# The first four feature pairs of each feed-forward layer as two 512-wide projections in two halves, in a four-layer decoder trunk

## The chip, the cores and the metric

The kernel is one program on one core of a Trainium2 chip. It takes one sequence of 256 tokens with 1024 channels through four residual layers. The metric is the device time of one execution in microseconds (us), lower is better. The kernel before takes 1203.94 us (median of 3 runs, 1202.83 to 1204.53).

The engines named here: TensorE (PE in the rows; PEld is its weight load), VectorE (DVE), ScalarE (ACT), GpSimd (POOL) and SyncE (SP, which issues the loads). Each works its own instructions off in order and waits on semaphores for the others.

## The reference, cut to what matters

Four layers, each a token mixer (attention, spatial gating, state-space, attention) and a feed-forward part. The change is in the feed-forward part:

```python
def conv_gated_ffn(xn, w_up, conv_w, conv_b, w_down):      # xn 256 x 1024, w_up 1024 x 5632
    h = causal_depthwise_conv(xn @ w_up, conv_w, conv_b)   # 3 taps over the tokens, per feature
    a, g = jnp.split(h, 2, axis=-1)                        # 2816 + 2816 features
    return (jax.nn.silu(g) * a) @ w_down                   # w_down 2816 x 1024

for i in range(DEPTH):
    xn = rmsnorm(x, norm_g[i, 0])
    m = ...                                                # mixer of this layer
    x = x + m
    x = x + conv_gated_ffn(rmsnorm(x, norm_g[i, 1]), ...)
return rmsnorm(x, final_norm_g)
```

## The kernel before

**Products in three.** Every weight chunk is a 128x2048 fp32 tile. ScalarE copies each half of it to a rounded high part `wh` (L85), VectorE subtracts to get the low part `wl` (L86), and a product is three matmuls: high by high, and the two mixed ones. The activations have such parts too, `xth` and `xtl` (1024 channels in 8 k-tiles by 256 tokens). `Weights` loads chunks ahead of use, and `step`, `prep_to` and `half_to` set how many are split ahead; the halves stand in the queues of ScalarE and VectorE between the other work.

**A feed-forward layer (class `FFN`).** Its 2816 feature pairs are 22 groups of 128 (`NM`), called u0 to u21 here; the chunk of a group holds the 128 `a` and 128 `g` columns for all 8 k-tiles. A group is projected *feature-major* (`proj_feat`): the weights are the stationary operand and the 256 tokens stream, 48 matmuls of 256 columns (L138 to L140), and the result, features by tokens, lies in one PSUM bank. Then `evac` takes it: two ScalarE activations with the middle tap and the bias (L432), four VectorE multiply-adds for the other two taps, reading the bank again (L436), then SiLU (L442), the product (L443) and the split for the next product (L212, L213). Each pair of groups is one chunk of the down product (d0 to d10, `down`, 24 matmuls of 512 columns, L146 to L148). The order of the body is u3, u4, u5, d0, u6, u7, d1, u8, u9, d2 and so on; `pend` delays the `evac` of a group to the round after its projection.

**The head.** The first three groups are projected *token-major* (`proj_tok`): the tokens of one block of 128 (block 0 or 1) are stationary and the 256 weight columns stream, so that block 0 can start while the norm of block 1 is still on its way. Two groups go to one bank (7 for block 0, 2 for block 1), the third to half of another (4 and 3). ScalarE copies these results to SBUF (`tk`, L388 and L389), and in the middle of u3 twelve transposes (L394) turn them into features by tokens in banks 4, 5 and 6, where `evac` finds them as it would u-groups.

**PSUM.** There are eight banks. Banks 0 to 3 are the accumulators of the down product from d0 on; banks 4 to 7 take the groups: group u*a* from u3 on goes to bank 4 + *a* mod 4, so u3 7, u4 4, u5 5, u6 6, u7 7. A matmul or transpose into a bank waits until the last reader of its former contents is done, and for a group that is the last of its four multiply-adds.

**Around the head.** `K.run` runs `tail(1)` of the phase before, the norm of block 1 (Square on ScalarE L165, power on GpSimd L177, scale on VectorE L169), then `head(0)`, which after its second chunk calls the transposes of block 1 (`xt_tr`, L193) and their evacuation (L199, L200), two more chunks are split, `head(1)`, one more chunk, and `body`. The attention phase already has a head of the other kind (`proj_half`, L236): 512 columns of half of the k-tiles per chunk.

The state-space layer (`S5`) uses `FFN.head` and `FFN.transposes` for its own input product.

Of the kernel before, what the change touches and what calls it, by code (L numbers as in the profile page):

```python
# [8 lines left out]
F32 = mybir.dt.float32  # L9
F32R = mybir.dt.float32r  # L10
BF16 = mybir.dt.bfloat16
AF = mybir.ActivationFunctionType
# [3 lines left out]
D = 1024  # L16
EPS = 1e-6
NM = 22
# [334 lines left out]
class FFN(Phase):  # L353
# [10 lines left out]
    def open(self):  # L364
        self.tmp = self.pool("ffn", 3)
        self.nc.scalar.preload_act_table_set("silu_and_others")
        self.cw = self.tmp.tile([128, 2, NM, 4], F32, tag="cw", bufs=1, name="cw")
        self.nc.sync.dma_start(self.cw[:, :, :, :], self.k.ins["conv"][self.i])
        self.bg = self.k.s5.stage(self.tmp) if self.k.s5 and self.k.s5.done else iter(())
        self.gt = {}  # L370
        self.acc = [[self.k.bank(2 * b + h) for h in range(2)] for b in range(2)]
        self.resid = self.k.add_acc(self.acc)
        self.hb = [(7, 4), (2, 3)]

    def head(self, b, mid):
        k = self.k
        if b == 0:
            self.hn = [k.w.take() for _ in range(3)]
        for c in range(3):
            p = k.bank(self.hb[b][c // 2])  # L380
            k.proj_tok(self.hn[c], b, p[:, 256 * (c % 2):256 * (c % 2) + 256])
            if c == 1:
                mid()
        if b == 0:
            self.tk = []
        tk = k.xn_p.tile([128, D], F32, tag="xn", name="tk")
        self.tk.append(tk)
        self.nc.scalar.activation(tk[:, 0:512], k.bank(self.hb[b][0]), AF.Copy)  # L388
        self.nc.scalar.activation(tk[:, 512:768], k.bank(self.hb[b][1])[:, 0:256], AF.Copy)  # L389

    def transposes(self, m, p):
        for b in range(2):
            for s in range(2):
                self.nc.tensor.transpose(p[:, 256 * s + 128 * b:256 * s + 128 * b + 128],  # L394
                                         self.tk[b][:, 256 * m + 128 * s:256 * m + 128 * s + 128],
                                         self.k.ident[:, :])

    def body(self):
        k, w = self.k, self.k.w
        pend = []  # L400
        for kind, a in self.order()[3:-3]:
            n = w.take()
            if kind == "u":
                p = k.bank(4 + a % 4)
                k.proj_feat(n, p, 0)
                if a == 3:
                    for m in range(3):
                        self.transposes(m, k.bank(4 + m))
                        pend.append((m, k.bank(4 + m)))
                k.proj_feat(n, p, 1)  # L410
                e = [(a, p)]
            else:
                k.down(self.gt[a], n, self.acc, (0, 1), a == 0, False)
                e = []
            self.evac(pend)
            pend = e
            w.step()
            for _ in range(1 + (kind == "d" and a % 2)):
                next(self.bg, None)
        self.evac(pend)  # L420
        for _ in self.bg:
            pass
# [339 lines left out]
class S5(Phase):  # L762
# [340 lines left out]
    def open(self):  # L1103
# [12 lines left out]
        nc.gpsimd.memset(self.kk[0][:, :, :, :], 0.0)  # L1116
        self.gt = {}

    def head(self, b, mid):
        FFN.head(self, b, mid)  # L1120
        if b == 0:
            k, w = self.k, self.k.w
            w.prep_to(w.use + 3)
            w.dma_to(w.use + 9)
            self.t0 = k.big.tile([128, D], F32, tag="gb", name="t0")
            for r in range(2):
                self.nc.sync.dma_start(self.t0[:, 512 * r:512 * r + 512], self.d_t[r][:, 0:512])
        else:
            self.k.w.prep_to(self.k.w.use + 6)

    def body(self):
        k, nc, w = self.k, self.nc, self.k.w
        ut = k.pst[:, 4:8, :].rearrange("p b (a t) -> p (b a) t", a=2)
        n = w.take()
        k.proj_feat(n, k.bank(7), 0)
        for m in range(3):
            FFN.transposes(self, m, k.bank(4 + m))
        k.proj_feat(n, k.bank(7), 1)
        tabs = [w.take() for _ in range(5)]
        TT = []  # L1140
        for i, tag in enumerate(("xth", "xtl")):
            t = k.big.tile([128, 2048], F32, tag=tag, name=f"T{i}")
# [149 lines left out]
        n = w.take()  # L1292
# [41 lines left out]
def pack(x, norm_g, final_norm_g, sb_w_qkv, sb_w_o, sg_w_in, sg_norm_g, sg_w_s, sg_b, sg_w_o,  # L1334
         ssm_w_in, ssm_lam_re, ssm_lam_im, ssm_log_dt, ssm_b_re, ssm_b_im, ssm_c_re, ssm_c_im,
         ssm_d, ssm_w_glu, ffn_w_up, ffn_conv_w, ffn_conv_b, ffn_w_down):

    c = np.ascontiguousarray
    a = {}
    a["x"] = x.reshape(2, 128, D)  # L1340
    a["g"] = np.concatenate([norm_g.reshape(8, D), final_norm_g.reshape(1, D), sg_norm_g.reshape(1, D)])
    a["up"] = c(ffn_w_up.reshape(4, 8, 128, 2, NM, 128).transpose(0, 4, 2, 1, 3, 5)).reshape(4, NM, 128, 2048)
    a["down"] = c(ffn_w_down.reshape(4, ND, 2, 128, D).transpose(0, 1, 3, 2, 4)).reshape(4, ND, 128, 2048)
    cv = np.concatenate([ffn_conv_w, ffn_conv_b[:, None]], axis=1)
    a["conv"] = c(cv.reshape(4, 4, 2, NM, 128).transpose(0, 4, 2, 3, 1))
    w = sb_w_qkv.reshape(2, 8, 128, 3, 8, 128)
    a["wqk"] = c(w[:, :, :, 0:2].transpose(0, 4, 2, 1, 3, 5)).reshape(2, 8, 128, 2048)
    w = sb_w_qkv[:, :, 2048:].reshape(2, 2, 4, 128, 2, 512)
    a["wv"] = c(w.transpose(0, 4, 1, 3, 2, 5)).reshape(2, 4, 128, 2048)
    a["wo"] = c(sb_w_o.reshape(2, 4, 2, 128, D).transpose(0, 1, 3, 2, 4)).reshape(2, 4, 128, 2048)  # L1350
    w = sg_w_in.reshape(8, 128, 2, 1024)
    a["sgu"] = c(w[:, :, 0].reshape(8, 128, 4, 2, 128).transpose(2, 1, 0, 3, 4)).reshape(4, 128, 2048)
    a["sgv"] = c(w[:, :, 1].reshape(2, 4, 128, 2, 512).transpose(3, 0, 2, 1, 4)).reshape(4, 128, 2048)
    a["sgo"] = c(sg_w_o.reshape(4, 2, 128, D).transpose(0, 2, 1, 3)).reshape(4, 128, 2048)
    a["sgws"] = c(sg_w_s[0].transpose(2, 0, 1))
    a["sgb"] = sg_b.reshape(1, D)
    w = ssm_w_in.reshape(8, 128, 4, 2, 128)
    a["ssin"] = c(w.transpose(2, 1, 0, 3, 4)).reshape(4, 128, 2048)
    w = ssm_w_glu.reshape(4, 2, 128, 2, 2, 512)
    a["glu"] = c(w.transpose(4, 0, 2, 1, 3, 5)).reshape(8, 128, 2048)  # L1360
    p = [ssm_lam_re[0], ssm_lam_im[0], np.broadcast_to(ssm_log_dt[0][:, None], (64, 64))]
    a["spar"] = c(np.stack([v.reshape(32, 128).T for v in p], axis=1))
    p = (ssm_b_re[0], ssm_b_im[0], ssm_c_re[0].transpose(0, 2, 1), ssm_c_im[0].transpose(0, 2, 1))
    a["sbc"] = c(np.stack([v.reshape(32, 2, 64, 16).transpose(1, 2, 0, 3) for v in p], axis=2)).reshape(128, 4, 512)
    v = np.stack([v.reshape(32, 2, 64, 16).transpose(1, 3, 0, 2) for v in p[:2]], axis=2).reshape(32, 2, 2048)
    a["sbt"] = c(np.tile(v, (4, 1, 1)))
    a["sd"] = c(ssm_d.reshape(8, 4, 32).transpose(1, 0, 2))
    a["e32"] = np.tile(np.eye(32, dtype=np.float32), (4, 1))
    i = np.arange(128)
    v = np.stack([i // 16 % 2, i // 64], axis=1)  # L1370
    a["own"] = c(np.stack([v[:, n] == g for n in range(2) for g in range(2)], axis=1).astype(np.float32))
    a["le"] = (i[:, None] <= i[None, :]).astype(np.float32)
    ge = (i[:, None] >= i[None, :]).astype(np.float32)
    one = np.ones((128, 128), np.float32)
    a["tri"] = np.concatenate([-ge, -one, np.float32(-1e30) * np.eye(128, dtype=np.float32), ge, ge], axis=1)
    a["ident"] = np.eye(128, dtype=np.float32)
    return a
# [28 lines left out]
```

## Time and profile before

| | |
|---|---|
| time, median of 3 runs | 1203.94 us |
| profiled execution: its own time | 1204.05 us |
| its span, first to last instruction | 1202.3 us |
| TensorE busy (matmul) | 1180.3 us, 98% |
| VectorE busy | 892.8 us, 74% |
| ScalarE busy | 709.4 us, 59% |
| feature-major matmuls of 256 columns (L138 to L140) | 4656, 283 to 284 ns each from start to modelled end |
| matmuls of 512 columns of the down products and their like (L146 to L148 on `gh`, `gl`) | 1536, 389 to 393 ns each |
| weights read | 222.27 MB from HBM, 196 GB/s over the span |

A matmul's duration in the profile runs to its modelled end and overlaps the next; what a stream of them costs is read from the distance between starts in the timeline. The number in brackets at the end of a timeline row is how long the engine had been idle before it, and which instruction ended that. Rows of equal instructions that follow each other are merged, with their count behind x.

### The profile page before, as it was taken

Reading aid. Unit: us, or ns where it says so; the run is one execution under the profiler, and the core shown is the slowest. Engines: PE = TensorE matmul, PEld = TensorE weight load, DVE = VectorE, ACT = ScalarE, POOL = GpSimd, SP = SyncE. Lnnn points to the kernel's source line nnn. Section 1 sums busy time; section 2 is a strip of 40 time slices with the busy share of each in tenths; the row PEclk is TensorE's granted clock in tenths of the full one; section 3 lists DMA queues with packets and bytes.
Section 4 is the critical chain, followed back from the end, with each engine's and each line's share of the span. In section 5 each row is a group of like instructions: output and inputs, shape, how many; then the busy total and the mean of one; then the engine's idle time right before and its main releaser. Section 6 shows DMA issues by size and latency. Waiting matters only on the chain. (4 is left out here: it accounts for less than half of the span.)

```text
span 1202.3 us, 22001 instructions
## 1 busy us (share of the span) xinstructions
PE 1180.3 (98%) x9076; PEld 1078.8 (90%) x9076; DVE 892.8 (74%) x1273; ACT 709.4 (59%) x1080; POOL 150.8 (13%) x293
## 2 busy tenths in 40 slices
PE   9999999999999999999987999999999999999997
PEld 5898999999898999999976899999988989999996
DVE  6665689799767699899569759777765656886673
ACT  6565576557564564667466657555545655665551
POOL 3894000000186001000100000000000000000000
PEclk9999999999999999999999999999999999999999
DMA  7633368787655456677762746644535333564530
GB/s 276 229 107 123 138 217 284 231 308 250 247 210 188 154 220 220 226 265 263 315 246 72 267 150 218 227 176 175 200 139 205 106 124 122 202 240 178 208 123 35
DMA packets 49416, 236.94 MB, mean 197 GB/s; under 512 B 14882, under 2 KB 15778, under 8 KB 24099
## 3 DMA queue, kind: packets, MB, share of 16 engines
q1 hardware_dynamic: 46066, 223.21, 51.6%
q0 software_dynamic: 3104, 12.06, 2.5%
q8 instruction: 71, 1.16, 0.4%
q14 instruction: 31, 0.25, 0.1%
q10 hardware_dynamic: 144, 0.26, 0.1%
HBM read 222.27 MB, written 13.24 MB: 196 GB/s over the span
## 5 line engine op out<-in xcount | busy, mean ns | idle before, releaser
L86 DVE TENSOR_TENSOR wl<-raw,wh 128x1024 fp32r<-128x1024 f32 x343 | 412.3, 1227 | 56.6 <-ACT wh L85 56.6
L138 PE MATMUL pst<-xth,wh 128*128 128x256 f32 x1552 | 441.0, 284 | 0.0
L139 PE MATMUL pst<-xtl,wh 128*128 128x256 f32 x1552 | 439.1, 283 | 0.0
L140 PE MATMUL pst<-xth,wl 128*128 128x256 f32 x1552 | 439.1, 283 | 0.0
L85 ACT ACTIVATE wh<-raw 128x1024 fp32r<-128x1024 f32 x343 | 349.4, 1048 | 8.4 <-DMA raw<-in_up_dram 4.2
L138 PEld LDWEIGHTS pst<-xth,wh 128*128 128x128 f32 x1552 | 297.7, 192 | 2.3
L139 PEld LDWEIGHTS pst<-xtl,wh 128*128 128x128 f32 x1552 | 297.8, 192 | 1.2
L140 PEld LDWEIGHTS pst<-xth,wl 128*128 128x128 f32 x1552 | 297.7, 192 | 0.0
L436 DVE SCALAR_TENSOR_TENSOR y<-pst,cw,y 128x255 f32<-128x255 f32 x352 | 160.7, 479 | 72.8 <-ACT y L432 66.6
L146 PE MATMUL pst<-wh,gh 128*128 128x512 f32 x512 | 201.3, 393 | 0.0
L147 PE MATMUL pst<-wl,gh 128*128 128x512 f32 x512 | 199.8, 390 | 0.0
L148 PE MATMUL pst<-wh,gl 128*128 128x512 f32 x512 | 199.4, 389 | 0.0
L432 ACT ACTIVATE y<-pst,cw 128x256 f32<-128x256 f32 x176 | 88.2, 557 | 69.4 <-PE pst L140 64.8
L148 PEld LDWEIGHTS pst<-wh,gl 128*128 128x128 f32 x512 | 96.1, 188 | 20.4
L146 PEld LDWEIGHTS pst<-wh,gh 128*128 128x128 f32 x512 | 96.2, 188 | 19.4 <-issue 0.3
L147 PEld LDWEIGHTS pst<-wl,gh 128*128 128x128 f32 x512 | 96.3, 188 | 18.4 <-DVE wl L86 0.2
L147 PE MATMUL pst<-wl,xth 128*128 128x256 f32 (+1 forms) x336 | 105.5, 314 | 1.3 <-DVE wl L55 1.0
L146 PE MATMUL pst<-wh,xth 128*128 128x256 f32 (+1 forms) x336 | 106.1, 316 | 0.0
L148 PE MATMUL pst<-wh,xtl 128*128 128x256 f32 (+1 forms) x336 | 105.4, 314 | 0.0
L177 POOL TENSOR_TENSOR r<-m,mhalf 128x1 f32<-128x1 f32 x20 | 11.1, 554 | 741.0 <-DVE m L175 732.5
L212 ACT ACTIVATE gh<-y 128x256 fp32r<-128x256 f32 x88 | 36.1, 418 | 75.2 <-DVE y L443 75.2
L442 ACT ACTIVATE y<-y 128x256 f32<-128x256 f32 x88 | 36.3, 419 | 73.7 <-DVE y L436 73.7
(173 smaller groups left out, 1203.0 us busy)
## 6 DMA issues: line engine op xcount, KB each, us to landing
raw<-in_up_dram SPq DMA_DIRECT2D x88, 1024.0 KB, 4.9
raw<-in_down_dram SPq DMA_DIRECT2D x44, 1024.0 KB, 4.9
raw<-in_wqk_dram SPq DMA_DIRECT2D x16, 1024.0 KB, 5.1
raw<-in_wo_dram SPq DMA_DIRECT2D x8, 1024.0 KB, 4.8
raw<-in_glu_dram SPq DMA_DIRECT2D x8, 1024.0 KB, 6.7
raw<-in_wv_dram SPq DMA_DIRECT2D x7, 1024.0 KB, 6.0
gb<-in_g_dram SPq DMA_DIRECT2D x8, 512.0 KB, 5.7
d_gt<-gf POOLq DMA_DIRECT2D x4, 1024.0 KB, 7.4
```

The lines of the kernel that those rows point to most:

```text
L85: nc.scalar.activation(h[:, s], r[:, s], AF.Copy)
L86: nc.vector.tensor_tensor(out=l[:, s], in0=r[:, s], in1=h[:, s], op=ALU.subtract)
L138: nc.tensor.matmul(out, h[:, cols], xh, start=first, stop=False, skip_group_check=True)
L139: nc.tensor.matmul(out, h[:, cols], xl, start=False, stop=False, skip_group_check=True)
L140: nc.tensor.matmul(out, l[:, cols], xh, start=False, stop=last, skip_group_check=True)
L146: nc.tensor.matmul(out, ah, h[:, cols], start=first, stop=False, skip_group_check=True)
L147: nc.tensor.matmul(out, ah, l[:, cols], start=False, stop=False, skip_group_check=True)
L148: nc.tensor.matmul(out, al, h[:, cols], start=False, stop=last, skip_group_check=True)
L212: self.nc.scalar.activation(g[0][:, j], src, AF.Copy)
L432: nc.scalar.activation(y[:, cs], p[:, cs], AF.Identity, scale=cw[:, s, m, 2:3], bias=cw[:, s, m, 3:4])
L436: nc.vector.scalar_tensor_tensor(y[:, o + tap:o + 256], p[:, o:o + 256 - tap], cw[:, s, m, 2 - tap:3 - tap], y[:, o + tap:o + 256], ALU.mu ...
L442: nc.scalar.activation(y[:, 256:512], y[:, 256:512], AF.Silu)
```

## The change

The head of a feed-forward layer takes the first *four* groups token-major, as two blocks of 512 columns (groups 0 and 1, groups 2 and 3), each in two chunks: chunk 0 and 1 hold the k-tiles 0 to 3 and 4 to 7 of the first block, chunk 2 and 3 of the second (`pack` lays the weights out so). `head` runs chunks 0 to 2 with `proj_half`, 12 matmuls of 512 columns each per token block, and copies the finished bank (7 or 2) to `tk` after the second. The fourth chunk, in the place where u3's chunk was, is run in `body` by `rest`, for block 0 (bank 4) and block 1 (bank 3). Between the two stand the transposes of groups 0 and 1 into banks 5 and 6; those of groups 2 and 3 into banks 4 and 5 stand in the middle of u4. The bank of a later group changes: u4 takes bank 7, and from u5 on group u*a* takes 4 + (*a* - 3) mod 4, so u5 6, u6 7, u7 4. `evac` takes groups 0 and 1 after the fourth chunk, 2 and 3 after u4, 4 after u5. The state-space layer keeps the old head under the name `narrow`.

```diff
+        self.vb = [(7, 4), (2, 3)]
     def head(self, b, mid):
         k = self.k
         if b == 0:
             self.hn = [k.w.take() for _ in range(3)]
+            self.tk = []
         for c in range(3):
-            p = k.bank(self.hb[b][c // 2])
-            k.proj_tok(self.hn[c], b, p[:, 256 * (c % 2):256 * (c % 2) + 256])
+            k.proj_half(self.hn[c], c % 2, b, k.bank(self.vb[b][c // 2]))
             if c == 1:
                 mid()
-        ...
-        self.nc.scalar.activation(tk[:, 0:512], k.bank(self.hb[b][0]), AF.Copy)
-        self.nc.scalar.activation(tk[:, 512:768], k.bank(self.hb[b][1])[:, 0:256], AF.Copy)
+                self.tk.append(k.xn_p.tile([128, D], F32, tag="xn", name="tk"))
+                self.nc.scalar.activation(self.tk[b][:, 0:512], k.bank(self.vb[b][0]), AF.Copy)
+    def rest(self, n, b, out):
+        p = self.k.bank(self.vb[b][1])
+        self.k.proj_half(n, 1, b, p)
+        self.nc.scalar.activation(out, p, AF.Copy)
...
     def body(self):
+        def part(m, bank):
+            self.transposes([t[:, 256 * m:256 * m + 256] for t in self.tk], k.bank(bank))
+            pend.append((m, k.bank(bank)))
         for kind, a in self.order()[3:-3]:
             n = w.take()
-            if kind == "u":
-                p = k.bank(4 + a % 4)
+            if kind == "u" and a == 3:
+                self.rest(n, 0, self.tk[0][:, 512:1024])
+                part(0, 5)
+                part(1, 6)
+                self.rest(n, 1, self.tk[1][:, 512:1024])
+                e = []
+            elif kind == "u":
+                p = k.bank(7 if a == 4 else 4 + (a - 3) % 4)
                 k.proj_feat(n, p, 0)
-                if a == 3:
-                    for m in range(3):
-                        self.transposes(m, k.bank(4 + m))
-                        pend.append((m, k.bank(4 + m)))
+                if a == 4:
+                    part(2, 4)
+                    part(3, 5)
                 k.proj_feat(n, p, 1)
                 e = [(a, p)]
...
+    w = ffn_w_up.reshape(4, 2, 4, 128, 2, NM, 128)[:, :, :, :, :, 0:4].reshape(4, 2, 4, 128, 2, 2, 2, 128)
+    a["up"][:, 0:4] = w.transpose(0, 5, 1, 3, 2, 6, 4, 7).reshape(4, 4, 128, 2048)
```

Line numbers behind the edit grow by 13: L432, L436 and L443 of before are L445, L449 and L456 of the changed kernel. In the rows of the order below a number behind `wh_`, `wl_` or `raw_` only tells one weight chunk from another.

ScalarE in the last feed-forward layer, from the evacuation of block 1's transposes on, before:

```order
L199 ACTIVATE xth<-pst 128x4x128 x2
L388 ACTIVATE tk<-pst 128x512
L389 ACTIVATE tk<-pst 128x256
L85 ACTIVATE wh_10770<-raw_10592 128x1024 x2
L85 ACTIVATE wh_10778<-raw_10612 128x1024 x2
L388 ACTIVATE tk<-pst 128x512
L389 ACTIVATE tk<-pst 128x256
L85 ACTIVATE wh_10861<-raw_10776 128x1024 x2
L432 ACTIVATE y<-pst,cw 128x256 x6
L85 ACTIVATE wh_10950<-raw_10784 128x1024
```

and in the changed kernel:

```order
L199 ACTIVATE xth<-pst 128x4x128 x2
L386 ACTIVATE tk<-pst 128x512
L85 ACTIVATE wh_10457<-raw_10316 128x1024 x2
L85 ACTIVATE wh_10465<-raw_10336 128x1024 x2
L386 ACTIVATE tk<-pst 128x512
L85 ACTIVATE wh_10511<-raw_10463 128x1024 x2
L392 ACTIVATE tk<-pst 128x512 x2
L445 ACTIVATE y<-pst,cw 128x256 x4
L85 ACTIVATE wh_10567<-raw_10471 128x1024
```

The two copies of `rest` (L392) now stand directly ahead of the first evacuation (L445); the second of them reads the product of block 1 with the fourth chunk.

VectorE in the same layer, from the end of the first evacuation's multiply-adds on, before (twelve of them end in the first row):

```order
L436 SCALAR_TENSOR_TENSOR y<-pst,cw,y 128x254
L86 TENSOR_TENSOR wl_10951<-raw_10784,wh_10950 128x1024
L443 TENSOR_TENSOR y<-y 128x256 x3
L86 TENSOR_TENSOR wl_10951<-raw_10784,wh_10950 128x1024
L213 TENSOR_TENSOR gl<-y,gh 128x256 x3
L86 TENSOR_TENSOR wl_10975<-raw_10867,wh_10974 128x1024 x2
L436 SCALAR_TENSOR_TENSOR y<-pst,cw,y 128x255
```

and in the changed kernel (eight end in the first row, eight follow in the last rows):

```order
L449 SCALAR_TENSOR_TENSOR y<-pst,cw,y 128x254
L86 TENSOR_TENSOR wl_10568<-raw_10471,wh_10567 128x1024
L456 TENSOR_TENSOR y<-y 128x256 x2
L86 TENSOR_TENSOR wl_10568<-raw_10471,wh_10567 128x1024
L213 TENSOR_TENSOR gl<-y,gh 128x256 x2
L86 TENSOR_TENSOR wl_10586<-raw_10517,wh_10585 128x1024 x2
L449 SCALAR_TENSOR_TENSOR y<-pst,cw,y 128x255
L449 SCALAR_TENSOR_TENSOR y<-pst,cw,y 128x254
```

Groups that were taken as 3, 1 and 1 are now taken as 2, 2 and 1; up to the last multiply-add of group 4 the same kinds stand there in the same numbers.

TensorE in the same layer, the end of d0 and the start of u6, with the engines that each row waits for, before:

```order
L146 MATMUL pst<-wh_10950,gh 128x512
L147 MATMUL pst<-wl_10951,gh 128x512
L148 MATMUL pst<-wh_10950,gl 128x512
L138 MATMUL pst<-xth,wh_10974 128x256 [waits Activation_49]
L139 MATMUL pst<-xtl,wh_10974 128x256
```

and in the changed kernel:

```order
L146 MATMUL pst<-wh_10567,gh 128x512
L147 MATMUL pst<-wl_10568,gh 128x512
L148 MATMUL pst<-wh_10567,gl 128x512
L138 MATMUL pst<-xth,wh_10585 128x256 [waits DVE_49,Activation_49]
L139 MATMUL pst<-xtl,wh_10585 128x256
```

u6's first matmul has a wait on VectorE that it did not have: its bank was group 2's and is now group 4's.

## Rows read from the trace of the kernel before

**Rows 1.** The page: busy time and share of the span; a group's busy, mean ns, idle.
```profile
PE 1180.3 (98%) x9076; PEld 1078.8 (90%) x9076; DVE 892.8 (74%) x1273; ACT 709.4 (59%) x1080; POOL 150.8 (13%) x293
...
L138 PE MATMUL pst<-xth,wh 128*128 128x256 f32 x1552 | 441.0, 284 | 0.0
```

**Rows 2.** Timeline of TensorE, last feed-forward layer: start, us, instruction, count.
```profile
1003.11 0.48 PE L146 MATMUL pst<-wh,gh 128*128 128x512 f32 x1
...
1005.93 0.28 PE L146 MATMUL pst<-wh,xth 128*128 128x256 f32 x1
...
1011.68 1.04 PE L193 MATMUL pst<-ident,xn 128*128 128x128 f32 x8
...
1026.94 1.47 PE L394 MATMUL pst<-ident,tk 128*128 128x128 f32 x12
1028.17 0.36 PE L138 MATMUL pst<-xth,wh 128*128 128x256 f32 x1
...
1042.65 0.40 PE L146 MATMUL pst<-wh,gh 128*128 128x512 f32 x1
...
1048.12 0.28 PE L138 MATMUL pst<-xth,wh 128*128 128x256 f32 x1
```

**Rows 3.** Timeline of TensorE, head of the second attention layer (`proj_half`).
```profile
886.69 0.39 PE L146 MATMUL pst<-wh,xth 128*128 128x512 f32 x1
...
892.14 1.04 PE L193 MATMUL pst<-ident,xn 128*128 128x128 f32 x8
892.93 0.47 PE L146 MATMUL pst<-wh,xth 128*128 128x512 f32 x1
...
903.92 0.28 PE L138 MATMUL pst<-xth,wh 128*128 128x256 f32 x1
```

**Rows 4.** Timeline of VectorE, last feed-forward layer; in brackets idle before, and releaser.
```profile
1025.63 2.36 DVE L86 TENSOR_TENSOR wl<-raw,wh 128x1024 fp32r<-128x1024 f32 x2 [4.01 <-ACT wh L85]
1028.69 5.54 DVE L436 SCALAR_TENSOR_TENSOR y<-pst,cw,y 128x255 f32<-128x255 f32 x12 [0.70 <-ACT y L432]
1034.15 1.22 DVE L86 TENSOR_TENSOR wl<-raw,wh 128x1024 fp32r<-128x1024 f32 x1
...
1040.70 1.91 DVE L436 SCALAR_TENSOR_TENSOR y<-pst,cw,y 128x255 f32<-128x255 f32 x4
...
1045.47 1.91 DVE L436 SCALAR_TENSOR_TENSOR y<-pst,cw,y 128x255 f32<-128x255 f32 x4
```

**Rows 5.** Timelines, TensorE's last 512-column matmul ahead of a head, then ScalarE rows.
```profile
696.68 0.39 PE L148 MATMUL pst<-wh,gl 128*128 128x512 f32 x1
...
697.11 0.60 ACT L1314 ACTIVATE gate<-pst 128x512 f32<-128x512 f32 x1 [1.54 <-PE pst L148]
...
703.30 1.09 ACT L199 ACTIVATE xth<-pst 128x512 fp32r<-128x512 f32 x2 [2.08 <-PE pst L193]
704.27 0.60 ACT L388 ACTIVATE tk<-pst 128x512 f32<-128x512 f32 x1
...
1027.63 2.84 ACT L432 ACTIVATE y<-pst,cw 128x256 f32<-128x256 f32 x6 [1.09 <-issue]
```

**Rows 6.** Critical chain in the state-space layer: start, us, what; then a stretch's busy.
```profile
659.20 0.69 DVE x L1192
659.90 0.04 issue
659.94 1.08 PE pst L1227 x61
...
650.00:660.00 10.00, 7.09 (x112) 5.56 (x104) 9.79 (x11) 3.65 (x4) 0.00 (x0) 1.00 0.30 107
```

**Rows 7.** Timeline of VectorE, first feed-forward layer.
```profile
168.05 0.44 DVE L982 STREAM_TRANSPOSE wt<-spar 128x256 f32<-128x256 f32 x1
168.41 1.87 DVE L436 SCALAR_TENSOR_TENSOR y<-pst,cw,y 128x255 f32<-128x255 f32 x4
```

**Rows 8.** Timelines, third feed-forward layer: the head's start, and the norm of block 1.
```profile
696.91 0.28 PE L146 MATMUL pst<-wh,xth 128*128 128x256 f32 x1
...
700.89 1.42 DVE L169 SCALAR_TENSOR_TENSOR xn<-x,r,gb 128x512 f32<-128x512 f32 x2 [0.73 <-POOL r L177]
```

**Rows 9.** A stretch further on, PE, PEld, DVE, ACT, POOL busy (count), clock.
```profile
1079.00:1096.00 17.00, 17.00 (x122) 16.04 (x121) 11.90 (x19) 9.44 (x15) 0.00 (x0) 1.00 0.50 185
```

More of the change, by code (lines that the diff above doesn't have):

```diff
@@ L372, in open @@
         self.resid = self.k.add_acc(self.acc)
-        self.hb = [(7, 4), (2, 3)]
+        self.vb = [(7, 4), (2, 3)]
     def head(self, b, mid):
@@ L378, in head, with transposes @@
             self.hn = [k.w.take() for _ in range(3)]
+            self.tk = []
         for c in range(3):
-            p = k.bank(self.hb[b][c // 2])
-            k.proj_tok(self.hn[c], b, p[:, 256 * (c % 2):256 * (c % 2) + 256])
+            k.proj_half(self.hn[c], c % 2, b, k.bank(self.vb[b][c // 2]))
             if c == 1:
                 mid()
[L384 to L387, printed above, removed]
-        self.nc.scalar.activation(tk[:, 0:512], k.bank(self.hb[b][0]), AF.Copy)
-        self.nc.scalar.activation(tk[:, 512:768], k.bank(self.hb[b][1])[:, 0:256], AF.Copy)
-    def transposes(self, m, p):
+                self.tk.append(k.xn_p.tile([128, D], F32, tag="xn", name="tk"))
[4 more added lines that the diff above has]
+        self.nc.scalar.activation(out, p, AF.Copy)
+    def transposes(self, tk, p):
         for b in range(2):
@@ L394, in transposes @@
                 self.nc.tensor.transpose(p[:, 256 * s + 128 * b:256 * s + 128 * b + 128],
-                                         self.tk[b][:, 256 * m + 128 * s:256 * m + 128 * s + 128],
-                                         self.k.ident[:, :])
+                                         tk[b][:, 128 * s:128 * s + 128], self.k.ident[:, :])
     def body(self):
@@ L1117, in open, with narrow, transposes @@
         self.gt = {}
+    def narrow(self, b, mid):
+        k = self.k
+        if b == 0:
+            self.hn = [k.w.take() for _ in range(3)]
+        for c in range(3):
+            p = k.bank(self.hb[b][c // 2])
+            k.proj_tok(self.hn[c], b, p[:, 256 * (c % 2):256 * (c % 2) + 256])
+            if c == 1:
+                mid()
+        if b == 0:
+            self.tk = []
+        tk = k.xn_p.tile([128, D], F32, tag="xn", name="tk")
+        self.tk.append(tk)
+        self.nc.scalar.activation(tk[:, 0:512], k.bank(self.hb[b][0]), AF.Copy)
+        self.nc.scalar.activation(tk[:, 512:768], k.bank(self.hb[b][1])[:, 0:256], AF.Copy)
+    def transposes(self, m, p):
+        for b in range(2):
+            for s in range(2):
+                self.nc.tensor.transpose(p[:, 256 * s + 128 * b:256 * s + 128 * b + 128],
+                                         self.tk[b][:, 256 * m + 128 * s:256 * m + 128 * s + 128],
+                                         self.k.ident[:, :])
     def head(self, b, mid):
-        FFN.head(self, b, mid)
+        self.narrow(b, mid)
         if b == 0:
@@ L1136, in body @@
         for m in range(3):
-            FFN.transposes(self, m, k.bank(4 + m))
+            self.transposes(m, k.bank(4 + m))
         k.proj_feat(n, k.bank(7), 1)
```

## The prediction

> **What bounds the kernel now.** I read the page first: TensorE is busy 98% of the span, and its commonest group, the feature-major matmuls, has no idle time ahead of it [rows 1]. So inside the feed-forward layers nothing but TensorE's own stream sets the time, and a change there is worth what it takes out of that stream, as long as no other engine becomes late. Next I read the timeline of TensorE through one head and the first rounds of the body, to get the distance between starts, which is what a matmul costs in a stream. I use the last layer; all four have the same pattern. All times below count from the start of the head's first matmul, 1005.93 [rows 2]. On that count the transposes of block 1 start at 5.75, the twelve transposes of `tk` at 21.01, d0 at 36.72 and u6 at 42.19. Last I read VectorE beside it: from its first multiply-add at 22.76 on it works without a pause to the last one of group 4, 1045.47 + 1.91 = 1047.38, which is 41.45 [rows 4]. TensorE does not wait for this: u6 goes to the bank of group 2, which has long been read.
>
> **TensorE's own work.** Removed per layer: 144 token-major and 48 feature-major matmuls of 256 columns. 48 of them took 1011.68 - 1005.93 = 5.75 us, so 0.1198 each [rows 2], and 192 take 23.00. Added: 96 matmuls of 512 columns. 24 of that kind took 892.14 - 886.69 = 5.45 us, 0.2271 each [rows 3], and 96 take 21.80. Also added are four transposes, 1.23 / 12 = 0.10 each [rows 2], 0.41 together. The net is 0.79 us less per layer, 3.2 us in four.
>
> [...]
>
> **What is late next.** Two things move together. First, `rest` for block 1 stands ahead of the first evacuation, and ScalarE takes its queue in order: it copies that product before it starts on group 0, though group 0's transposes are done 2.8 us earlier. Second, the banks: u5 and the transposes of group 3 go into banks 6 and 5, where groups 1 and 0 have just been, and u6 goes into bank 7, u4's, one product and one d-step after u4. So TensorE now waits for VectorE to get through group 4.
>
> When VectorE can start: two chunks 5.45, eight transposes 0.79, then 60 wide matmuls, of which 48 took 903.92 - 892.93 = 10.99 and 12 more take 2.73 [rows 3]. That is 19.96. Eight transposes, 0.79, make 20.75, and the twelve matmuls of `rest` for block 1 behind them 2.82, as twelve behind transposes did between 1003.11 and 1005.93 [rows 2]. So the fourth chunk ends at 23.57. Its last matmul starts 0.23 before that, ScalarE starts 697.11 - 696.68 = 0.43 after that start (23.77), and the next instruction behind a copy of this size follows half of 704.27 - 703.30, so 0.49, later (24.26) [rows 5]. VectorE's first multiply-add came 1028.69 - 1027.63 = 1.06 after ScalarE's first evacuation [rows 4, 5], so now at 25.32. Before it was 22.76: VectorE starts 2.56 later.
>
> How long it needs to group 4: the same 20 multiply-adds, 6 half splits, 4 products and 4 subtractions stand between, grouped 2, 2, 1 in place of 3, 1, 1. Before this took 1047.38 - 1028.69 = 18.69 without a pause [rows 4], and ScalarE, idle for part of that time, supplied it. I take the same 18.69, so group 4 is done at 44.01. TensorE follows 0.05 behind (659.89 to 659.94) [rows 6]: u6 starts at 44.06.
>
> When TensorE would be there: 23.57, half of u4 (24 x 0.12 = 2.88), four transposes to 26.86. Bank 5 is free when group 0's four multiply-adds are through, 25.32 + 1.91 + 0.05 = 27.28, so a first wait of 0.4. Four transposes, 0.41, the other half of u4, 2.88, u5 5.75 and d0 5.47 [rows 2] give 41.79. The second wait is 44.06 - 41.79 = 2.3 us, and it swallows the first. Behind u6's first matmul TensorE's whole queue waits.
>
> **The sum.** u6 starts at 44.06 in place of 42.19, so each layer loses 1.87 us. In the first feed-forward layer VectorE has an extra transposition for the state-space tables in that stretch, 168.41 - 168.05 = 0.36 [rows 7], which had cover before and has none now: 2.2 there. 3 x 1.87 + 2.2 = 7.8 us. Nothing gives it back: TensorE had no waits behind u6 in a feed-forward layer that could shrink. Nor does the wait repeat: in a later round of 17 us VectorE is busy for 11.90 [rows 9], so it catches up by 5 us a round, and the banks come round after four groups again. The profiled execution took 1204.05, 0.11 above the median; on the median the sum is 1203.94 + 7.8 = 1211.7.
>
> **Edits at nothing.** The head's first two chunks are the cover for the norm of block 1, and they shrink from 5.75 to 5.45. The tightest layer is the third: its head starts at 696.91 and the norm is done at 700.89 + 1.42 = 702.31 [rows 8], against 702.36; without cover it would cost what it is late, under 0.1. The copies of `tk` grow from two of 0.60 and two of 0.38 to four of 0.60, on ScalarE, which is idle 41% of the span [rows 1]; the one that matters is priced above. Two weight splits on ScalarE no longer stand behind a copy that waits for chunk 2, so they come earlier, ahead of need in both kernels. The loads are as many and as large, and the state-space layer issues what it issued.
>
> The trace shows no matmul that waits at u6, so the wait is bounded from both sides: from none (u6 at 41.79, a gain of 0.40 per layer) to the wait that follows if ScalarE is late as well, by one weight split of 1.0 to 1.2 us in the chain [rows 4] (45.2, a loss of 3.0). I take 2.3, since the chain that it rests on is one unbroken stretch of rows. [...]
>
> **Rivals.** *No hold at u6*: VectorE reaches group 4 by 41.7, and only TensorE's sum and the first wait count, 0.40 gained per layer, 1203.9 - 1.6 = 1202.3. For it: VectorE idles 4 us and more in the head [rows 4]. Against it: that idle time lies ahead of the evacuation, which cannot start before `rest` is done, and behind it there is none. Chance 0.07. *Faster*: neither bank holds TensorE; group 0 is read by 26.8 and group 4 by 41.4, and the whole 0.79 per layer stays: 1203.9 - 3.2 = 1200.8. It decides if VectorE starts 2.6 us earlier than I have it, that is if ScalarE's evacuation of group 0 does not queue behind the copy for block 1. The order has it behind. Chance 0.04. *A longer chain*: products and splits in twos leave gaps on VectorE (a product must wait for SiLU, which waits for its group's multiply-adds), one split's length per layer: 4 x 1.1 more, 1216.1. Against it: ScalarE's instructions come out ahead of VectorE's at each of these places when I place them by their rows, by 0.1 at the nearest. Chance 0.05.
>
> **How the numbers follow.** The forecast has 0.84, with its own range 1208.5 to 1214.5 (0.7 either way per layer). The range given, 1207.0 to 1215.5, leaves out the two faster rivals (0.11) and a part of the longer chain. No change means within 0.2% (2.4 us, about what a measurement of this kernel can tell): 1201.5 to 1206.3 holds the first rival and a little of the forecast's low end, 0.08; faster 0.04; slower 0.88.
>
> **What would show it.** After: the timeline of TensorE has, four times, an idle time of about 2.3 us ahead of u6's first matmul, put down to the multiply-add, and one of about 0.4 ahead of the transposes of group 3. From the head's first matmul to u6 it is 44.1 in three layers and 44.4 in the first. The fourth chunk ends at 23.6; the 512-column matmuls in the head stand 0.227 apart; VectorE's first multiply-add comes at 25.3, and the last of group 4 is 18.7 later. The second attention layer and the state-space layer keep their lengths. I am wrong if u6 starts within 0.4 of 42.19, or if a wait of the same kind stands at u7 or later.

## The result and the profile after

The changed kernel takes 1215.12 us (median of six runs, 1214.07 to 1218.48), the kernel before, measured beside it, 1203.91 (median of six): a ratio of 1.0097, 95% interval 1.0087 to 1.0107. It is slower, as forecast, by 11.2 us in place of 7.8. The profiled execution took 1217.58 us (span 1215.8), 13.5 more than that of before. One run of the kernel before beside experiments 1 to 4 took 1634.34 us at a mean granted clock of 0.654; it is a slow run and left out of what follows.

The page and the waits of TensorE answer to [rows 1]. First the page; in the third group of columns stands the idle time ahead of the group:

```profile
PE 1183.4 (97%) x8708; PEld 1064.4 (88%) x8708; DVE 892.7 (73%) x1273; ACT 711.2 (58%) x1080; POOL 151.8 (12%) x293
...
L138 PE MATMUL pst<-xth,wh 128*128 128x256 f32 x1488 | 425.3, 286 | 8.4 <-DVE y L449 8.4
```

Then the list of TensorE's waits (in all, times, longest):

```profile
PE pst L138 <- DVE y L449: 8.4, 4, 2.3
...
PE pst L146 <- ACT gh L1274: 1.7, 1, 1.7
PE pst L193 <- DVE xn L169: 1.7, 1, 1.7
...
PE pst L398 <- DVE y L449: 1.3, 4, 0.3
```

The group that had no idle time now has 8.4 us of it, in four waits for the multiply-adds (L449, before L436). The timeline of TensorE in the last layer, which answers to [rows 2], shows where. The head starts at 1015.97; L193 are the transposes of block 1, L398 those of `tk`:

```profile
1015.97 0.39 PE L146 MATMUL pst<-wh,xth 128*128 128x512 f32 x1
...
1021.41 1.03 PE L193 MATMUL pst<-ident,xn 128*128 128x128 f32 x8
...
1035.92 1.03 PE L398 MATMUL pst<-ident,tk 128*128 128x128 f32 x8
...
1039.53 0.28 PE L138 MATMUL pst<-xth,wh 128*128 128x256 f32 x1
...
1042.40 0.60 PE L398 MATMUL pst<-ident,tk 128*128 128x128 f32 x4
1043.33 0.63 PE L398 MATMUL pst<-ident,tk 128*128 128x128 f32 x4 [0.33 <-DVE y L449]
...
1052.42 0.40 PE L146 MATMUL pst<-wh,gh 128*128 128x512 f32 x1
...
1060.08 0.36 PE L138 MATMUL pst<-xth,wh 128*128 128x256 f32 x1 [2.02 <-DVE y L449]
...
1061.22 0.33 PE L138 MATMUL pst<-xth,wh 128*128 128x256 f32 x1
1061.35 0.41 PE L139 MATMUL pst<-xtl,wh 128*128 128x256 f32 x1
1061.57 0.42 PE L140 MATMUL pst<-xth,wl 128*128 128x256 f32 x1
```

And VectorE beside it, which answers to [rows 4]:

```profile
1041.27 3.73 DVE L449 SCALAR_TENSOR_TENSOR y<-pst,cw,y 128x255 f32<-128x255 f32 x8 [6.66 <-ACT y L445]
...
1050.79 3.71 DVE L449 SCALAR_TENSOR_TENSOR y<-pst,cw,y 128x255 f32<-128x255 f32 x8
...
1058.03 1.90 DVE L449 SCALAR_TENSOR_TENSOR y<-pst,cw,y 128x255 f32<-128x255 f32 x4
```

From the head's first matmul it is 23.56 us to u4, 25.30 to VectorE's first multiply-add, 43.96 to the end of group 4, 44.11 to u6. Then something comes that the forecast didn't have: in this layer, 1.1 us after u6 has begun, matmuls of 256 columns start 0.22 us apart instead of 0.12. The clock (the column with 1.00, after the busy times of PE, PEld, DVE, ACT and POOL) in stretches of 2 us:

```profile
1058.00:1060.00 2.00, 0.05 (x1) 0.00 (x0) 1.93 (x6) 1.50 (x3) 0.00 (x0) 1.00 0.72 197
1060.00:1062.00 2.00, 1.92 (x14) 1.95 (x14) 2.00 (x3) 1.05 (x3) 0.00 (x0) 0.83 0.78 328
1062.00:1064.00 2.00, 2.00 (x11) 2.00 (x11) 1.97 (x5) 1.81 (x4) 0.00 (x0) 0.50 0.14 25
1064.00:1066.00 2.00, 2.00 (x16) 2.00 (x16) 1.96 (x4) 1.25 (x2) 0.00 (x0) 0.82 0.94 381
1066.00:1068.00 2.00, 2.00 (x19) 2.00 (x19) 2.00 (x4) 1.79 (x3) 0.00 (x0) 1.00 0.31 127
```

In this layer the granted clock fell to 0.50 after the wait, while TensorE was already busy again (11 matmuls in 2 us in place of 19), and rose some 3 us later. In the first layer, where u6 starts at 177.52, it had fallen just before the wait ended:

```profile
177.30:177.50 0.20, 0.00 (x0) 0.01 (x1) 0.20 (x2) 0.20 (x1) 0.00 (x0) 0.50 1.06 451
177.50:180.50 3.00, 2.98 (x14) 3.00 (x15) 3.00 (x5) 2.05 (x5) 0.00 (x0) 0.50 0.93 385
```

A layer can be measured from its head's first matmul to that of the next layer (the last one to its last matmul). Before, the feed-forward layers took 189.78, 189.78, 189.78 and 188.66 us, the state-space layer 111.60. Now it is 193.49, 193.27, 191.79, 192.14 and 112.56; the other two layers kept their lengths. So the 13.5 us of this execution are: the later u6, 2.25 + 1.93 + 1.93 + 1.92 = 8.0; u6 and u7 together, 12.98, 13.07, 11.58 and 13.06 us in place of 11.51, so 4.7; and 1.0 in the state-space layer; with 0.1 less ahead of the first layer. The forecast had the first term alone. What the median's 11.2 us are made of can't be read in this way, since the faster executions have no trace.

### The profile page after: what moved, and what is told of

Read it like the earlier page. It is cut to its first block, busy times and chain, and to the rows that moved or that the text cites. A ratio compares the mean times of both kernels' runs of the same rounds, so it can differ in the third digit from the quotient of the medians.

```text
span 1215.8 us, 21263 instructions
## 1 busy us (share of the span) xinstructions
PE 1183.4 (97%) x8708; PEld 1064.4 (88%) x8708; DVE 892.7 (73%) x1273; ACT 711.2 (58%) x1080; POOL 151.8 (12%) x293
## 5 line engine op out<-in xcount | busy, mean ns | idle before, releaser
L138 PE MATMUL pst<-xth,wh 128*128 128x256 f32 x1488 | 425.3, 286 | 8.4 <-DVE y L449 8.4
L139 PE MATMUL pst<-xtl,wh 128*128 128x256 f32 x1488 | 423.1, 284 | 0.0
L140 PE MATMUL pst<-xth,wl 128*128 128x256 f32 x1488 | 423.0, 284 | 0.0
L138 PEld LDWEIGHTS pst<-xth,wh 128*128 128x128 f32 x1488 | 287.5, 193 | 12.3 <-ACT y L455 10.0
L139 PEld LDWEIGHTS pst<-xtl,wh 128*128 128x128 f32 x1488 | 287.6, 193 | 1.2
L140 PEld LDWEIGHTS pst<-xth,wl 128*128 128x128 f32 x1488 | 287.6, 193 | 0.0
L449 DVE SCALAR_TENSOR_TENSOR y<-pst,cw,y 128x255 f32<-128x255 f32 x352 | 160.6, 479 | 97.0 <-ACT y L445 90.8
L445 ACT ACTIVATE y<-pst,cw 128x256 f32<-128x256 f32 x176 | 88.1, 556 | 65.4 <-PE pst L140 65.4
L147 PE MATMUL pst<-wl,xth 128*128 128x512 f32 (+1 forms) x272 | 101.0, 371 | 1.2 <-DVE wl L55 1.0
L146 PE MATMUL pst<-wh,xth 128*128 128x512 f32 (+1 forms) x272 | 102.1, 375 | 0.0
L148 PE MATMUL pst<-wh,xtl 128*128 128x512 f32 (+1 forms) x272 | 101.0, 371 | 0.0
```

The costliest lines, as they stand in the source:

```text
L138: nc.tensor.matmul(out, h[:, cols], xh, start=first, stop=False, skip_group_check=True)
L139: nc.tensor.matmul(out, h[:, cols], xl, start=False, stop=False, skip_group_check=True)
L140: nc.tensor.matmul(out, l[:, cols], xh, start=False, stop=last, skip_group_check=True)
L146: nc.tensor.matmul(out, ah, h[:, cols], start=first, stop=False, skip_group_check=True)
L147: nc.tensor.matmul(out, ah, l[:, cols], start=False, stop=False, skip_group_check=True)
L148: nc.tensor.matmul(out, al, h[:, cols], start=False, stop=last, skip_group_check=True)
```

## The experiments

Diffs are against the changed kernel, and layer lengths are counted as above. Experiments 1 to 4 were run several times, the others once each. The kernel before, run beside 1 to 4, took 1203.15 to 1205.79 us in 25 executions and 1210.17 in one, so a single time can be several us off, and experiments 5 to 12 are read by their layers.

**1. u6 in a free bank.** With the banks in another order u6 goes to bank 4.

```diff
-                p = k.bank(7 if a == 4 else 4 + (a - 3) % 4)
+                p = k.bank((7, 6, 4, 5)[a % 4])
```

> The changed kernel with other banks from u6 on: u4 7, u5 6, u6 4, u7 5, u8 7, u9 6 and so on, so that u6 follows group 2 and not group 4. Theory (the wait for bank 7 costs 1.9 to 2.2 us per layer, and the clock that falls behind it another 1.5 us in most layers): no wait ahead of u6, granted clock 1.00 there, u6 and u7 together 11.5 us; from the head's first matmul to u6 41.8 us (42.19 before); 1202.3 us in all, give or take 1. Rival (the matmuls of u6 and u7 are slowed by loads and VectorE at work beside them, not by the wait): the wait goes, but u6 and u7 stay at 13 us, 1208.

Measured: 1205.81 us (median of 11, 1204.82 to 1210.04), ratio 1.002 (1.0011 to 1.0029). u6 starts at 41.91 to 41.93 in the four layers without a wait, and u6 and u7 take 11.51 in each: with the wait gone, so is the slow clock. The 0.3 us at bank 5 stay. Three layers take 189.52, 189.52 and 188.39, 0.26 less than before, but the second takes 191.32, and that was not foreseen; nor was the state-space layer (116.93 in the profiled execution, 1210.04 us, where the clock fell three times; its mean over the execution was 0.993, before 0.998). So the time missed the forecast of 1201.3 to 1203.3.

**2. The same, and the transposes of groups 2 and 3 behind all of u4.**

```diff
+                k.proj_feat(n, p, 1)
                 if a == 4:
                     part(2, 4)
                     part(3, 5)
-                k.proj_feat(n, p, 1)
```

> As the first, and the transposes of groups 2 and 3 stand behind the second half of u4 in place of the middle, so that bank 5 is read before they come. Theory: no wait in the feed-forward layers at all, 41.4 us from the head's first matmul to u6, TensorE's whole saving of 0.79 us per layer, 1200.8 us. Rival (the later transposes make VectorE late for d1 or a later bank): a new wait of 0.5 us or more between u5 and u8, 1202.5 or more.

Measured: 1203.54 us (11 runs, 1202.71 to 1207.69), ratio 1.0 (0.9992 to 1.0009). No waits of either kind, and three layers at 188.99, 189.00 and 187.87, 0.79 less than before. So the wait of the rival did not come between u5 and u8, but the time is the rival's all the same (1202.5 or more): the second layer takes 190.64, longer than before again. Its TensorE timeline has waits at its end, where the last group's products are awaited:

```profile
572.96 0.50 PE L146 MATMUL pst<-wh,gh 128*128 128x512 f32 x1 [0.78 <-ACT gh L212]
...
573.99 0.50 PE L148 MATMUL pst<-wh,gl 128*128 128x512 f32 x1 [0.29 <-DVE gl L213]
```

**3. VectorE started earlier.** The banks of the changed kernel; groups 0 and 1 are evacuated ahead of block 1's second half, and the transposes moved as in 2.

```diff
                 part(1, 6)
+                self.evac(pend)
+                pend = []
                 self.rest(n, 1, self.tk[1][:, 512:1024])
```

> The changed kernel's banks, but the evacuation of groups 0 and 1 is issued ahead of the fourth chunk's product for block 1 and its copy, and the transposes of groups 2 and 3 come behind the second half of u4. Theory (VectorE is late because ScalarE's evacuation queues behind that copy): VectorE's first multiply-add at 21.7 us from the head's first matmul in place of 25.3, group 4 done at 40.4 to 41.4, u6 at 41.4 with a wait under 0.3; 1200.8 to 1202 us. Rival (VectorE's work up to group 4 takes as long wherever it starts, since it waits for group 3's or group 4's product): u6 stays at 43 or later, 1207 or more.

Measured: 1201.52 us (11 runs, 1200.21 to 1202.29), ratio 0.9977 (0.9967 to 0.9987): this version (version 3 below) beats both kernels, the one before by 2.2 us. Its VectorE and then its TensorE in the last layer, whose head starts at 1004.47:

```profile
1026.16 3.73 DVE L451 SCALAR_TENSOR_TENSOR y<-pst,cw,y 128x255 f32<-128x255 f32 x8 [3.04 <-ACT y L447]
...
1043.13 1.90 DVE L451 SCALAR_TENSOR_TENSOR y<-pst,cw,y 128x255 f32<-128x255 f32 x4
```

```profile
1045.64 0.39 PE L148 MATMUL pst<-wh,gl 128*128 128x512 f32 x1
1045.87 0.28 PE L138 MATMUL pst<-xth,wh 128*128 128x256 f32 x1
```

VectorE begins 21.69 after the head's start, in place of 25.30, is through group 4 at 40.56, and u6 follows d0 at 41.40 with no idle time, though it goes to the same bank 7 as in the changed kernel. All four layers are 0.79 us shorter than before, which is the sum for TensorE's own work in the prediction.

**4. The wait filled.** Eight 512-column matmuls that nothing reads go into bank 4, free there, ahead of u6.

```diff
+                if a == 6:
+                    for _ in range(8):
+                        self.nc.tensor.matmul(k.bank(4), k.xth[:, 0, 0:128], w.hl[n][0][:, 0:512], start=True, stop=True)
                 k.proj_feat(n, p, 0)
```

> The changed kernel with eight extra matmuls of 512 columns (1.8 us) into bank 4, which is free then, right ahead of u6; they compute nothing that is used. The wait for VectorE ends when it ended, but TensorE works through most of it. Theory (the clock falls because TensorE stands still for 2 us): granted clock 1.00 behind it, u6 and u7 together 11.5 us in all four layers, u6 at 44.1 us from the head's first matmul as in the changed kernel; 1211.7 to 1212.7 us, as forecast for the wait alone. Rival (u6 and u7 are slow for another reason): 13 us in most layers, 1215 or more.

Measured: 1214.22 us (median of 4, 1213.84 to 1217.11), ratio 1.0093 (1.0079 to 1.0106). u6 starts at 44.45, 44.12, 44.13 and 44.12 as if nothing had been filled in, since VectorE is no earlier; TensorE idles 0.6 us at most, and u6 and u7 take 11.58 to 11.59 in all four layers. So the slow clock of the changed kernel belongs to TensorE's idle time and not to what VectorE, ScalarE or the loads do there. The times don't show it: 1211.7 to 1212.7 was forecast, and 1214.22, or 10.5 us over the kernel before, is close to the 11.2 of the changed kernel, with overlapping intervals. Three of these four runs took 1213.84 to 1214.39, three of the changed kernel's six 1214.07 to 1214.29. The profiled execution, at 1217.11, had three falls of the clock in the state-space layer instead (116.42 us; mean clock 0.993).

**5. The changed kernel again**, unaltered.

> The changed kernel once more, unaltered, in another execution. My theory: each of the four waits at u6 leaves the clock free to fall, and whether it does differs from one execution to the next. Then u6 starts at +44.4, +44.1, +44.1, +44.1 us from its head again, while u6 and u7 together take 11.5 us in some layers and 13.0 in others, not the same three layers as before; the time is 1212 to 1217.6 us, 1.5 per layer that falls. Rival: the fall belongs to the layer (what else runs there); then again layers one, two and four take 13.0 and the third 11.6, and the time is 1217.5. A second question is the boundary from the state-space layer to the third feed-forward layer, where the changed kernel lost 0.96 us: if the wait for the normalized tokens is 1.5 to 1.7 us again, it belongs to the change; if it is 0.3 to 0.9, it is the scatter of one transfer.

Measured: 1216.92 us. The four stretches behind u6, the clock in the third column from the right:

```profile
178.00:182.00 4.00, 4.00 (x36) 4.00 (x35) 3.93 (x9) 3.09 (x6) 0.00 (x0) 1.00 0.80 289
443.00:447.00 4.00, 4.00 (x24) 4.00 (x23) 3.93 (x8) 2.27 (x4) 0.00 (x0) 0.58 0.45 154
749.00:753.00 4.00, 4.00 (x36) 4.00 (x35) 3.93 (x9) 3.04 (x6) 0.00 (x0) 1.00 0.44 143
1060.50:1064.50 4.00, 4.00 (x23) 4.00 (x23) 3.93 (x8) 3.53 (x6) 0.00 (x0) 0.57 0.46 152
```

The offsets of u6 repeat (44.46, then 44.12 three times), the clock does not: this time it fell in the second and the fourth layer, and not in the first. So the fall is not bound to the layer alone. The wait for the normalized tokens at the end of the state-space layer is 1.4 us, after 1.7 in the first trace: between the two ranges given, and nearer to that of the change.

**6. Half of the wait filled**, with `range(4)` in the edit of 4.

> The changed kernel with four extra 512-column matmuls into the unused bank 4 ahead of u6 (eight in the earlier run), 4 x 0.227 = 0.9 us, so that TensorE idles 1.1 to 1.4 us in place of 2.0 to 2.3. They write numbers that nothing reads. u6 starts at +44.1 to +44.4 as before. If the fall of the clock needs a wait near the full length, u6 and u7 take 11.5 to 11.6 us in all four layers and the time is 1214, as with eight. If any wait of about a microsecond is enough, they take 13 us in two or more layers and the time is 1216 to 1218.

Measured: 1212.80 us. TensorE idles 1.44, 1.13, 1.12 and 1.12 us ahead of u6, u6 starts where it did, and u6 and u7 take 11.58 to 11.59 in each layer: no fall. This execution is the changed kernel without its slow clock in these layers, 1.1 us above the forecast.

**7. Version 3 with the banks of 1.**

> The mended version (first two groups evacuated ahead of block 1's second half, transposes of groups 2 and 3 after u4) with the rotated banks 7, 6, 4, 5 besides. My theory: with the rotated banks alone the second feed-forward layer waited 0.8 + 0.3 us at its end because VectorE's chain, which there also fills the state-space tables, ran late to the last group; with the chain begun 3.6 us earlier it is not late, whatever the banks. Then the second feed-forward layer takes 189.0 us from head to head as the others, and the time is 1201.5. Rival: the rotated order of the banks makes that wait by itself; then this layer takes 190.6 and the time is 1203.2.

Measured: 1203.32 us. The feed-forward layers take 188.99, 189.00, 188.99 and 187.88, and no wait stands at the second one's end: the bank order does not make it, the late chain does. VectorE also computes state-space tables in that layer and is busy for 165 of its 191 us (experiment 2; 139 in the third), so it has little time to catch up, and lateness that no longer stops TensorE at u6 comes back at the layer's end. The forecast of 1201.5 was missed by the state-space layer alone, 114.08 us with three falls of the clock (its mean 0.993).

**8. The early evacuation alone**, the transposes where the change has them.

> The changed kernel with one edit: groups 0 and 1 are evacuated ahead of block 1's second half; banks and the place of the transposes of groups 2 and 3 as the change has them. My theory: the late start of VectorE's chain was the whole cause of both waits. Then VectorE's first multiply-add starts at +21.7 us of the head (+25.3 in the changed kernel), the 0.3 us wait at bank 5 and the wait at u6 are both gone, u6 starts at about +41.4, each feed-forward layer takes 189.0 us, and the time is 1201.5. Rival: the early transposes need bank 5 before it is read; then 0.3 us per layer stays, the layers take 189.3 and the time is 1202.8.

Measured: 1209.41 us; neither theory had it. The wait at u6 is gone (43.03 to 43.11, on the heels of d0), but a wait of 1.40 to 1.48 us stands ahead of the transposes of groups 2 and 3, and a layer takes 190.7. First TensorE there, then ScalarE (L392 copies `tk`, L447 evacuates):

```profile
1038.64 0.88 PE L398 MATMUL pst<-ident,tk 128*128 128x128 f32 x6 [1.40 <-ACT tk L392]
```

```profile
1031.06 1.93 ACT L447 ACTIVATE y<-pst,cw 128x256 f32<-128x256 f32 x4
...
1035.03 0.42 ACT L457 ACTIVATE y<-y 128x256 f32<-128x256 f32 x1 [0.79 <-DVE y L451]
...
1037.35 0.75 ACT L212 ACTIVATE gh<-y 128x256 fp32r<-128x256 f32 x2 [0.95 <-DVE y L458]
1038.01 0.58 ACT L392 ACTIVATE tk<-pst 128x512 f32<-128x512 f32 x1
```

The copy of the fourth chunk now queues on ScalarE behind the whole evacuation of groups 0 and 1, which itself waits for VectorE twice, and the transposes need this copy. In version 3 they come one half of u4 later, which covers it.

**9. The later transposes alone**, the edit of 2 with the changed kernel's banks.

> The changed kernel with one edit: the transposes of groups 2 and 3 after both halves of u4 instead of between them. My theory: this takes away the 0.3 us at bank 5, and TensorE comes to u6 0.5 us earlier (+41.4), but VectorE's chain starts as late as before, ends group 4 at +44.0, and the wait at u6 grows to 2.65 us: a layer is 191.7 us, the sum 1211.5, and 1.5 us more for each layer in which the clock falls, which a longer wait makes no rarer (1211.5 to 1217.5). Rival: the early transposes are the cause of the chain's late start; then u6 starts at about +41.4 without a wait, the layers take 189.0 and the time is 1201.5.

Measured: 1216.65 us. The wait at bank 5 is gone, u6 starts at 44.45, 44.12, 44.11 and 44.12 as ever, and the wait there is 2.9 us in the first layer and 2.6 in the others: the chain of VectorE sets u6's start, not the place of the transposes. u6 and u7 take 13.07, 13.07, 11.59 and 11.58. Experiments 8 and 9 together show that version 3 needs both of its edits.

**10. The kernel before again.**

> The kernel before once more, unaltered, for the stages that the change doesn't touch. From head to head the state-space stage took 111.6 us in the profiled run of before, and 112.2 to 116.9 in six runs of changed kernels. If that is scatter of the stage (one transfer from memory, the clock within the stage), before shows it too: 112 us or more, and a wait for the normalized tokens at its end that is not 0.7 us; the time is 1204 to 1206. If it is due to the change, before takes 111.6 and waits 0.7 us again.

Measured: 1204.40 us. The state-space layer takes 111.08 us and waits 0.2 for the normalized tokens; but the clock fell in it twice, though the layer was no longer than in the first trace (111.60), where it did not fall. The first fall and a part of the second; below them the second place in the earlier execution of the same kernel:

```profile
627.30:630.60 3.30, 3.30 (x128) 3.30 (x132) 3.27 (x6) 0.49 (x1) 0.00 (x0) 0.50 0.02 5
644.50:647.50 3.00, 3.00 (x8) 2.31 (x7) 2.83 (x4) 2.41 (x4) 0.00 (x0) 0.50 0.01 3
```

```profile
644.50:647.50 3.00, 3.00 (x15) 2.44 (x14) 2.86 (x4) 1.58 (x3) 0.00 (x0) 1.00 0.00 0
```

**11. The changed kernel a third time.**

> The changed kernel a third time, unaltered, for more of its waits at u6. My theory: u6 starts at +44.1 to +44.5 us with a wait of 2.0 to 2.4 us in all four layers; which of them are followed by a fall of the clock (u6 and u7 together 13.0 us in place of 11.6) differs from run to run: between one and four here, 1213 to 1218 us. Rival: it belongs to the layer: it falls in the second and the last, which fell in both runs, never in the third.

Measured: 1217.04 us; u6 at 44.47, 44.12, 44.12, 44.13; falls in the second and the fourth layer. That is what the rival said. With the first trace and experiments 5 and 9, the second layer fell in four executions of four, the fourth in three, the first in two, the third in none: the layer matters, though it doesn't decide alone.

**12. A quarter of the wait filled**, with `range(2)`.

> The changed kernel with two extra 512-column matmuls into the unused bank 4 ahead of u6 (four and eight earlier), 2 x 0.227 = 0.45 us, so that TensorE idles 1.6 us in three layers and 1.9 in the first. They write numbers that nothing reads. u6 starts at +44.1 to +44.4 again. If only a wait of about 2 us lets the clock fall, u6 and u7 take 11.6 us in all layers and the time is 1212.8 to 1214.2. If a wait of 1.6 us is enough, they take 13 us in one layer or more, and the time is 1.5 us longer for each.

Measured: 1213.49 us; u6 and u7 take 11.58 to 11.59 in all four layers.

Together, by layer:

| Kernel | Idle ahead of u6, us | u6 and u7, us |
|---|---|---|
| Before, twice; experiments 1, 2, 3, 7, 8 | none | 11.51 |
| Eight filled in (4) | 0.6, then 0.2 to 0.3 | 11.59, 11.58, 11.58, 11.58 |
| Four filled in (6) | 1.4, 1.1, 1.1, 1.1 | 11.58, 11.58, 11.59, 11.58 |
| Two filled in (12) | 1.9, 1.6, 1.6, 1.6 | 11.58, 11.58, 11.59, 11.58 |
| Changed, profiled first | 2.3, 2.0, 2.0, 2.0 | 12.98, 13.07, 11.58, 13.06 |
| Changed, again (5) | 2.4, 2.0, 2.0, 2.0 | 11.58, 13.07, 11.58, 13.07 |
| Changed, a third time (11) | 2.4, 2.0, 2.0, 2.0 | 11.57, 13.07, 11.58, 13.05 |
| Later transposes alone (9) | 2.9, 2.6, 2.6, 2.6 | 13.07, 13.07, 11.59, 11.58 |

## Why the prediction was right in kind and too low

**TensorE's own work: right.** Its saving of 0.79 us per layer is what is left when nothing waits (experiments 3 and 7).

**What is late next: right.** The steps came out within 0.2 us: fourth chunk 23.56 (23.57 forecast), VectorE's first multiply-add 25.30 (25.32), group 4 done 43.96 (44.01), u6 44.11 (44.06) and 44.43 in the first layer (44.4), the first wait 0.33 (0.4). The wait at u6 was 2.2 in place of 2.3: d0 starts at 36.45 (36.32 by the sum) and takes 5.47, so TensorE was there at 41.92. The profile lists 2.0, since it counts idle time from the modelled end of the last matmul. That both causes named are real is shown one at a time: another bank takes the wait away (1), an earlier start of VectorE does too (3, 8), and an earlier or later arrival of TensorE leaves u6 where it is (4, 6, 9, 12). The sum of 7.8 us measured 8.0, and 8.3 with the slower first matmuls behind the waits.

**The failed step: the sum has nothing for the clock behind a wait.** That rested on one stretch of one execution, where the granted clock was 1.00 [rows 6]. The stretch was read rightly: TensorE had waited 2.2 us there, in the kernel before, and no fall followed:

```profile
659.94 1.10 PE L1227 MATMUL pst<-x,wh 128*32 128x64 f32 x64 [2.24 <-DVE x L1192]
```

It was one case, and no run shows a clock that stays up behind every such wait. In the changed kernel, three profiled executions had 12 waits of 2.0 to 2.4 us at u6, and 7 were followed by a fall of the clock to 0.50, at 1.4 to 1.5 us each: 2 to 3 falls and 3.0 to 4.4 us per execution. The experiments with the wait filled tie this to the idle time: none of their 12 waits of 0.2 to 1.9 us was followed by a fall. And the very stage that the argument came from showed the clock at 0.50 in the second execution of the kernel before (10): one execution without a fall had been taken for the rule.

The three traces are of executions at 1216.9 to 1217.6 us. On the median the falls weigh less: the changed kernel lost 11.2 us against the kernel before, the one with eight matmuls filled in 10.5. So of the 3.4 us between the forecast loss and the median, the falls behind u6 are about 0.7, the later u6 0.2 and the slower first matmuls 0.3; some 2 us are left, which is an estimate by difference; the state-space layer's 1.0 to 1.9 us (next paragraph) are most of it.

**A second failed step: "the state-space layer keep their lengths".** Before, it took 111.60 and 111.08 us; in the three executions of the changed kernel 112.56, 113.44 and 113.45. A part stands at its end. In the chain of waits, the last load that the third feed-forward layer's start hangs on, of the changed kernel and of before (10):

```profile
686.99 6.65 DMA raw<-in_up_dram
```

```profile
680.74 5.20 DMA raw<-in_up_dram
```

In all nine traces of changed kernels in which the first evacuation stands behind block 1's second half, this load takes 6.17 to 6.65 us; in the two of before and the three with the early evacuation, 5.11 to 5.69. So it goes with the late evacuation, and takes 0.5 to 1.5 us longer; what makes it longer there stays open. The rest, another wait and the clock within that layer, varies from execution to execution (111.1 to 116.9 in all). The number of falls does not explain it, with 111.08 us at two falls (10) and 112.56 at none (the changed kernel's first trace), and it stays open.

**The rivals.** *Faster* named the right condition, VectorE's earlier start, and experiment 3 met it: 1201.5 for 1200.8. *No hold at u6* is experiment 1 in three layers of four (0.26 gained for its 0.40); it left out that in the second layer VectorE cannot catch up. *A longer chain* would have given 1216.1, near the measured time, but the chain took 18.66 in place of 18.69: the right size for a wrong reason.

With the clock undisturbed in these layers the kernel took 1212.80 (6), 1213.49 (12) and 1214.22 (4, the median). The remaining 1.1 to 2.5 us over 1211.7 are, in the first two, the slower restart (0.3), 0.2 of the wait and the state-space layer (0.5 and 1.0 longer than in the first trace of before).

## What to carry to other kernels

When an edit makes a full engine wait, price the wait, and then ask what the engine does when it resumes; the clock behind a wait is a risk to be put into the range with its own chance (here a fall after 9 of 16 waits of 2.0 to 2.9 us, at 1.4 to 1.5 us each), and a single execution without a fall proves nothing. A wait that is taken away at one place can come back at the next where the late engine has no slack (in experiments 1 and 2 the second layer took 191.32 and 190.64 us, before 189.78), so look for the stage in which it also has other work. Before moving an instruction forward on an in-order queue, name what now stands behind it: experiment 8 freed one wait and made another, of 1.40 to 1.48 us.

## What was not expected of the hardware

The granted clock fell to 0.50 mostly not during a wait but up to 1.5 us after TensorE had resumed (once 0.3 us before), for about 3 us, and cost 1.4 to 1.5 us. At this place it did so after 9 of 16 waits of 2.0 to 2.9 us, in the first layer of the same program in one execution and not in the next, and after none of 12 waits of 0.2 to 1.9 us; yet in the state-space layer of the kernel before (10) it fell after single waits of at most 0.73 us and again after at most 1.64. No run here shows what else decides it, and which waits are followed by a fall stays open.
